# Two product groups at the start of a streaming-encoder step in full float32, their splits moved five groups later

## The chip, the core and the metric

The program runs on one core of a Trainium2 chip. The metric is device time in microseconds (us) from start to end of one execution; a smaller number is better. The engines named here are TensorE (PE in the profile; its weight loads stand apart as PEld), VectorE (DVE), ScalarE (ACT), GpSimd (POOL) and SyncE (SP, which issues most DMA transfers). Each engine works through its own instructions in the written order and waits where an instruction needs something that another engine or a transfer has not yet delivered.

## The reference

The reference is one inference step of a one-layer hybrid encoder on 1024 prompt tokens and 32 sample tokens (1056 in all), 1024 features wide, all in float32:

```python
h = rmsnorm(x, g_mix)
proj = h @ w_in
q, k, v, cb, cc, cx, ga, gc = jnp.split(proj, SPLITS, axis=-1)
y_attn = attend(q, k, v) @ w_attn_out          # stick-breaking attention, 8 heads of 64
conv_out, new_buf = causal_conv(cc * cx, conv_buf, conv_w)
y_conv = (cb * conv_out) @ w_conv_out
merged = jax.nn.sigmoid(ga) * y_attn + jax.nn.sigmoid(gc) * y_conv
x = x + merged @ w_o
f = jnp.square(jax.nn.relu(rmsnorm(x, g_ffn) @ w_up)) @ w_down
x = x + f
x = x + jax.nn.sigmoid(rmsnorm(x, g_ple) @ w_ple_gate) * (p @ w_ple)
```

The change lies in the first pieces of `h @ w_in`. The kernel multiplies `x * g_mix` with the weights and applies the row's norm to the result later, so the first products need only `x`, `g_mix` and `w_in`.

## The kernel before

**Split float32.** Nearly all large products are done in three fast products in place of a slow float32 one. An operand is split into a high part (written as `fp32r` by ScalarE) and a low part (the remainder, written as `fp32r` by VectorE). For each 128-feature piece TensorE then does high weight times high x (L371), high weight times low x (L372) and low weight times high x (L373), all added up in one PSUM tile. Those three lines are in `products`, and what it calls a group here is one call: 8 feature pieces, 24 matrix products of 128x128 weights with 264 tokens, one PSUM tile `ps_g`.

**The first stage.** `first_gates` (L1010 on) computes four output blocks of 128 columns for all 1056 tokens: `SETS[0]` (blocks 0 and 1, weights `i0`) and `SETS[1]` (weights `i1`). The tokens lie in four quarters of 264; quarters 0 and 1 are the first half (`near_` and `far_`), 2 and 3 the second half (`whole_`). That makes 16 groups, numbered 0 to 15 in this document as the loop's `n` has it: groups 0 and 1 are the two blocks of `i0` on quarter 0 (the near tokens), 2 and 3 on quarter 1 (the far tokens), 4 to 7 on quarters 2 and 3; groups 8 to 11 are `i1` on quarters 2 and 3, groups 12 to 15 `i1` on quarters 0 and 1.

**What feeds it.** SyncE loads, in this order: the first half of block 0's weights, the near tokens in four pieces of two features blocks each (the second half of block 0's weights after the second piece), the two halves of block 1's weights, the far tokens in four pieces, the second half of the tokens in four pieces, and whole weight blocks of the later sets (`fetch_in`, L115). The loop runs at record time, and the order in which it calls things is the order on each engine:

- `half_of(j, h)` splits one half of the weights of block `j`: a ScalarE cast (L1033) and a VectorE subtraction (L1034).
- `parts_x(h, c, fs)` splits token range `c` for the features blocks `fs`: per block one ScalarE scaling by `g_mix` that rounds (L693) and one VectorE remainder (L182, in the helper `mix`). On a quarter these are 128x264, on `whole_` 128x528.
- `out(s, i, t)` copies a finished PSUM tile to SBUF on ScalarE (L1017); it stands one group behind.
- From group 4 on the generator `sums_x` runs one step after each group; its first steps scale the second half of `x` in place (ScalarE, L701) and form differences (VectorE, also L182, named `x<-x` in the profile).
- At groups 6 and 7, `prepare_plain` splits the weights of `i1`: a ScalarE cast (L124) and a VectorE subtraction `wlo_i` (L125), each over a whole 128x1024 block. Group 8 is the first that uses them; its third product needs `wlo_i`.
- At group 8 `fetch_in(2)` and `prepare("i2")` come in: GpSimd forms four sums of weights (`steps` in `prepare`, all recorded under L252).

Ahead of group 0 TensorE does `IDLE` products of `ones` with `ones` (L1393, tile `ps_idle`) whose result nobody reads. Both weight and token tiles come from pools of fixed size; a load into a tile that was used before waits for its last reader.

## Time and profile before

| what | value |
|---|---|
| time, median of 3 runs | 1510.66 us (1510.4 to 1511.49) |
| the profiled execution's own time | 1511.53 us |
| its span, first to last instruction | 1509.8 us |
| TensorE busy in the span | 1494.7 us (99%) |
| VectorE, ScalarE, GpSimd busy | 1153.5, 791.5, 375.7 us |
| granted TensorE clock | 0.998 of full |

The prediction reads views of this one execution. The timeline gives, in order of time, rows of start, length, engine, source line, operation, `out<-in`, shape, how many equal ones were merged (x8), and in brackets how long the engine had been idle before and what ended that. A length is from the start of the first to the end of the last of a row; since an engine starts an instruction before the former one has fully ended, the distance from start to start is a little shorter than the length of one. The tile and line views give the smallest, median and largest duration of an instruction in nanoseconds and, for a DMA, the time from issue to landing. A row with `SPq` is the issue of a transfer, not the transfer.

### The profile page before, as it was taken

The page shows a single profiled execution, that of the slowest core. Times are in us where ns is not written, and L with a number is a line of the kernel's source. Part 1 is how long each engine was busy: PE and PEld are TensorE (multiplying, and loading weights), DVE is VectorE, ACT ScalarE, POOL GpSimd, SP SyncE. Part 2 cuts the span into 40 slices and gives each one's busy share as a digit, 9 for nine tenths or more (in the row PEclk, how much of TensorE's full clock was granted, in tenths as well). Part 3 has the DMA queues.
Part 4 walks back from the last instruction along what each step waited for, and adds up shares of the span by engine and source line. Part 5 has one row for each costly group of instructions (what it writes and reads, how often), then busy time and mean ns, then how long its engine had stood idle before and what let it go on. Part 6 is the DMA issues. An engine that isn't in the chain of part 4 may idle for free.

```text
span 1509.8 us, 29499 instructions
## 1 busy us (share of the span) xinstructions
PE 1494.7 (99%) x11580; PEld 1480.6 (98%) x11580; DVE 1153.5 (76%) x1624; ACT 791.5 (52%) x1567; POOL 375.7 (25%) x334
## 2 busy tenths in 40 slices
PE   9999999999999999999999999999999999999997
PEld 9999999999999999999999999999999999999997
DVE  7667689879578999876786676666689878879766
ACT  6654444445467767433475555555655433334655
POOL 1233335444121223003324433332000000000251
PEclk9999999999999999999999999999999999999999
DMA  6624425422678676654644334444879757855443
GB/s 245 211 73 170 163 64 198 154 84 96 220 247 276 182 170 143 220 196 162 234 163 149 136 137 150 157 150 157 312 281 289 244 187 239 295 186 166 141 129 123
DMA packets 116747, 275.52 MB, mean 182 GB/s; under 512 B 14048, under 2 KB 30048, under 8 KB 116608
## 3 DMA queue, kind: packets, MB, share of 16 engines
q1 hardware_dynamic: 112720, 260.44, 50.9%
q0 software_dynamic: 1728, 6.29, 2.5%
q10 hardware_dynamic: 2160, 6.91, 1.5%
q8 instruction: 91, 1.49, 0.4%
q14 instruction: 48, 0.39, 0.1%
HBM read 196.10 MB, written 85.88 MB: 187 GB/s over the span
## 4 chain that ended last, share of the span: by engine, by line
PE 92%; DVE 4%; DMA 1%; ACT 1%; issue 1%; SPq 0%; ACTq 0%; DVEq 0%
PE ps_dn L2000 6%; PE ps_dn L1999 6%; PE ps_dn L1998 6%; PE ps_A11i L371 4%; PE ps_A11i L372 4%; PE ps_A11i L373 4%; PE ps_A11u L372 4%; PE ps_A11u L371 4%; PE ps_A11u L373 4%; PE av L1278 2%; PE ps_S1i L373 2%; PE ps_S1i L372 2%; PE ps_S1i L371 2%; PE ps_wo L133 2%; PE ps_wo L135 2%; PE ps_wo L134 2%
## 5 line engine op out<-in xcount | busy, mean ns | idle before, releaser
L2000 PE MATMUL ps_dn<-fhP,wlo_dn 128*128 128x264 f32 x768 | 218.6, 285 | 0.0
L1999 PE MATMUL ps_dn<-flP,whi_dn 128*128 128x264 f32 x768 | 218.2, 284 | 0.2 <-DVE flP L1864 0.2
L1998 PE MATMUL ps_dn<-fhP,whi_dn 128*128 128x264 f32 x768 | 218.2, 284 | 0.0
L1999 PEld LDWEIGHTS ps_dn<-flP,whi_dn 128*128 128x128 f32 x768 | 144.4, 188 | 0.4 <-DVE flP L1864 0.4
L2000 PEld LDWEIGHTS ps_dn<-fhP,wlo_dn 128*128 128x128 f32 x768 | 144.5, 188 | 0.2 <-DVE wlo_dn L1848 0.2
L1998 PEld LDWEIGHTS ps_dn<-fhP,whi_dn 128*128 128x128 f32 x768 | 144.5, 188 | 0.0
L2213 POOL TENSOR_TENSOR xx<-xx,pgs 128x400 f32<-128x400 f32 (+1 forms) x17 | 20.0, 1183 | 281.4 <-DVE pgs L2212 281.4
L1223 DVE TENSOR_TENSOR_SCAN r<-r 128x128 f32<-128x128 f32 (+3 forms) x64 | 86.7, 1355 | 4.0 <-POOL r L1216 4.0
L371 PE MATMUL ps_A11i<-T,shS_i 128*128 128x264 f32 x288 | 82.5, 286 | 0.4 <-ACT u_i L515 0.4
L372 PE MATMUL ps_A11i<-T,shS_i 128*128 128x264 f32 x288 | 82.1, 285 | 0.0
L373 PE MATMUL ps_A11i<-T,slS_i 128*128 128x264 f32 x288 | 81.7, 284 | 0.0
L371 PE MATMUL ps_A11u<-T,shS_u 128*128 128x264 f32 x256 | 73.3, 286 | 0.0
L372 PE MATMUL ps_A11u<-T,shS_u 128*128 128x264 f32 x256 | 73.0, 285 | 0.0
L373 PE MATMUL ps_A11u<-T,slS_u 128*128 128x264 f32 x256 | 72.7, 284 | 0.0
L1216 POOL TENSOR_SCALAR_AFFINE_SELECT r<-r 128x128 f32<-128x128 f32 x64 | 35.8, 560 | 133.1 <-ACT r L1209 133.1
L1842 ACT CAST whi_dn<-raw_dn 128x1024 fp32r<-128x1024 f32 x31 | 32.6, 1052 | 66.2 <-PE ps_dn L1999 54.0
L135 PE MATMUL ps_wo<-mh,wlo_wo 128*128 128x352 f32 x192 | 62.0, 323 | 0.0
L1864 DVE TENSOR_TENSOR flP<-mrP,fhP 128x1056 fp32r<-128x1056 f32 x48 | 59.9, 1251 | 2.8 <-ACT fhP L1859 2.8
L134 PE MATMUL ps_wo<-ml,whi_wo 128*128 128x352 f32 x192 | 62.0, 323 | 0.0
L133 PE MATMUL ps_wo<-mh,whi_wo 128*128 128x352 f32 x192 | 61.7, 324 | 0.0
L250 DVE TENSOR_TENSOR slS_i<-s_i,shS_i 128x512 fp32r<-128x512 f32 x54 | 49.5, 917 | 13.1 <-ACT shS_i L191 12.8
L1263 DVE TENSOR_TENSOR at<-pa,at 128x512 fp32r<-128x512 f32 (+2 forms) x96 | 50.6, 548 | 11.4 <-ACT at L1262 10.6
(1704 smaller groups left out, 5794.8 us busy)
## 6 DMA issues: line engine op xcount, KB each, us to landing
raw_dn<-in_w_down_dram SPq DMA_DIRECT2D x59, 512.0 KB, 5.1
mrP<-mdT SPq DMA_DIRECT2D x32, 528.0 KB, 6.1
mdB<-m SPq DMA_DIRECT2D x48, 264.0 KB, 2.1
mrP<-mdB SPq DMA_DIRECT2D x24, 528.0 KB, 6.8
s<-gd SPq DMA_DIRECT2D x16, 528.0 KB, 5.3
mdT<-ta SPq DMA_DIRECT2D x32, 264.0 KB, 3.2
raw_pg<-in_w_ple_gate_dram SPq DMA_DIRECT2D x15, 512.0 KB, 3.5
gd<-m_i SPq DMA_DIRECT2D x12, 528.0 KB, 3.0
```

The lines of the kernel that those rows point to most:

```text
L133: nc.tensor.matmul(ps, wh, xh[k][:, cols], start=(k == order[0]), stop=False)
L134: nc.tensor.matmul(ps, wh, xl[k][:, cols], start=False, stop=False)
L135: nc.tensor.matmul(ps, wl, xh[k][:, cols], start=False, stop=(k == order[-1]))
L371: nc.tensor.matmul(p_, wh[:, k, :], h, start=new and n == 0, stop=False, **on)
L372: nc.tensor.matmul(p_, wh[:, k, :], l, start=False, stop=False, **on)
L373: nc.tensor.matmul(p_, wl[:, k, :], h, start=False, stop=z, **on)
L1223: nc.vector.tensor_tensor_scan(rev, rev, rev, 1.0, ALU.mult, ALU.bypass)
L1263: nc.vector.tensor_tensor(al, pt[:, :nb, :], ah.bitcast(F32), op=ALU.subtract)
L1864: dve(l, mraw.pop(v), opd[v].bitcast(F32), op=sub)
L1998: nc.tensor.matmul(ps, hi[:, j, :], oh, start=j == 0, stop=False)
L1999: nc.tensor.matmul(ps, hi[:, j, :], ol, start=False, stop=False)
L2000: nc.tensor.matmul(ps, lo[:, j, :], oh, start=False, stop=j == NP_ - 1)
```

## The change

Groups 0 and 1 no longer use split operands. A new function scales the near tokens on ScalarE into plain float32 tiles `xs`, and a second one multiplies these with the raw, unsplit weights in float32 products, 8 of them to a group. The splits of block 0's and 1's weights, and of the far tokens, are recorded at group 1, the far tokens now with the even feature blocks ahead of the odd ones. The near tokens are still split, since groups 12 to 15 use them, but at group 5. The idle products are 8, not 14.

```diff
-IDLE = 14
+IDLE = 8
...
+        xs = [blk(f"xs{h}", F32, [P, 4, TQ]) for h in range(2)]
+
+        def whole_x():
+            for f in range(8):
+                src = xw[0][f // 2][:, f % 2, near_]
+                nc.scalar.activation(xs[f // 4][:, f % 4, :], src, AF.Copy, scale=gmix[:, f : f + 1])
+
+        def whole_product(i):
+            p_ = group(f"ps_f{i}", TQ)
+            fs = (0, 2, 1, 3, 4, 5, 6, 7)
+            for f in fs:
+                w = raws["i0"][i][:, 4 * (f % 2) + f // 2, :]
+                nc.tensor.matmul(p_, w, xs[f // 4][:, f % 4, :], start=f == fs[0], stop=f == fs[-1])
+            return p_
...
+                whole_x()
+            elif n == 1:
                 half_of(0, 0)
-                parts_x(0, near_, (0, 1, 2, 3))
+                parts_x(0, far_, (0, 2, 4, 6))
                 half_of(0, 1)
-                parts_x(0, near_, (4, 5, 6, 7))
+                parts_x(0, far_, (1, 3, 5, 7))
                 half_of(1, 0)
                 half_of(1, 1)
-            elif n in (1, 3):
-                parts_x(n // 2, far_ if n == 1 else whole_)
+            elif n == 3:
+                parts_x(1, whole_)
+            elif n == 5:
+                parts_x(0, near_)
...
-            late.append(products(f"g{s_}{i}{t}", ((w[a], f"B1{c}"), (w[b], f"B2{c}")), quarters[t % 2]))
+            if n < 2:
+                late.append(whole_product(i))
+            else:
+                late.append(products(f"g{s_}{i}{t}", ((w[a], f"B1{c}"), (w[b], f"B2{c}")), quarters[t % 2]))
```

**ScalarE at the start of the program.** In the rows, `x00` to `x03` are the four pieces of the first half of the tokens (near and far columns of a piece have the same name), `x10` to `x13` those of the second half, `B11`, `B21` their split parts for even and odd feature blocks, `raw_i0_0` and `raw_i0_1` the weights of blocks 0 and 1. Before:

```order
L1033 CAST whi_i0_0_193<-raw_i0_0_88 128x512
L693 ACTIVATE B11_0_199<-x00_80,vecT_78 128x264
L693 ACTIVATE B21_00_202<-x00_80,vecT_78 128x264
...
L1033 CAST whi_i0_1_195<-raw_i0_1_89 128x512 x2
L693 ACTIVATE B11_0_199<-x00_80,vecT_78 128x264
L693 ACTIVATE B21_01_254<-x00_80,vecT_78 128x264
L693 ACTIVATE B11_1_205<-x01_81,vecT_78 128x264
...
L1017 COPY sg0_191<-ps_g000_227 128x264
L1017 COPY sg1_192<-ps_g010_270 128x264
L693 ACTIVATE B12_0_322<-x10_84,vecT_78 128x528
```

And now:

```order
L1026 ACTIVATE xs0_187<-x00_80,vecT_78 128x264 x2
...
L1026 ACTIVATE xs1_188<-x03_83,vecT_78 128x264 x2
L1048 CAST whi_i0_0_189<-raw_i0_0_88 128x512
L693 ACTIVATE B11_0_212<-x00_80,vecT_78 128x264
L693 ACTIVATE B11_1_215<-x01_81,vecT_78 128x264
L693 ACTIVATE B11_2_218<-x02_82,vecT_78 128x264
L693 ACTIVATE B11_3_221<-x03_83,vecT_78 128x264
L1048 CAST whi_i0_0_189<-raw_i0_0_88 128x512
L693 ACTIVATE B21_01_226<-x00_80,vecT_78 128x264
...
L1048 CAST whi_i0_1_191<-raw_i0_1_89 128x512 x2
L1017 COPY sg0_185<-ps_f0_201 128x264
```

The number of ScalarE instructions ahead of the splits of the second half (`B12_0`) is the same, 22 in all; the eight scalings into `xs` take the place of the eight near splits, and and the four even splits of the far tokens, one from each far piece, now stand ahead of the four odd ones and of three of the weight casts.

**VectorE between the second half's splits and the low part of the weights of `i1`.** Before:

```order
L182 SCALAR_TENSOR_TENSOR B22_3_343<-x13_87,vecT_78,B22_3_343 128x528
L182 SCALAR_TENSOR_TENSOR x10_84<-x10_84,vecT_78 128x528
L182 SCALAR_TENSOR_TENSOR x11_85<-x11_85,vecT_78 128x528
L182 SCALAR_TENSOR_TENSOR x12_86<-x12_86,vecT_78 128x528
L182 SCALAR_TENSOR_TENSOR x13_87<-x13_87,vecT_78 128x528
L182 SCALAR_TENSOR_TENSOR x10_84<-x00_80,vecT_78,x10_84 128x528
L182 SCALAR_TENSOR_TENSOR x11_85<-x01_81,vecT_78,x11_85 128x528
L125 TENSOR_TENSOR wlo_i1_0_461<-raw_i1_0_106,whi_i1_0_460 128x1024
```

And now:

```order
L182 SCALAR_TENSOR_TENSOR x11_85<-x11_85,vecT_78 128x528
L182 SCALAR_TENSOR_TENSOR B11_0_212<-x00_80,vecT_78,B11_0_212 128x264
...
L182 SCALAR_TENSOR_TENSOR B21_10_367<-x03_83,vecT_78,B21_10_367 128x264
L182 SCALAR_TENSOR_TENSOR x12_86<-x12_86,vecT_78 128x528
L182 SCALAR_TENSOR_TENSOR x13_87<-x13_87,vecT_78 128x528
L182 SCALAR_TENSOR_TENSOR x10_84<-x00_80,vecT_78,x10_84 128x528
L182 SCALAR_TENSOR_TENSOR x11_85<-x01_81,vecT_78,x11_85 128x528
L125 TENSOR_TENSOR wlo_i1_0_433<-raw_i1_0_106,whi_i1_0_432 128x1024
```

All eight low parts of the near tokens now stand between the second and the third difference of `sums_x`, ahead of `wlo_i` of group 8. From `wlo_i` on, the instructions of every engine stand in the order they had.

More of the change, by code (lines that the diff above doesn't have):

```diff
@@ L1035, in half_of @@
                     ws["i0"][f"A{j + 1}{h + 1}"] = hi, lo
+                whole_x()
+            elif n == 1:
                 half_of(0, 0)
-                parts_x(0, near_, (0, 1, 2, 3))
+                parts_x(0, far_, (0, 2, 4, 6))
                 half_of(0, 1)
-                parts_x(0, near_, (4, 5, 6, 7))
+                parts_x(0, far_, (1, 3, 5, 7))
                 half_of(1, 0)
                 half_of(1, 1)
-            elif n in (1, 3):
-                parts_x(n // 2, far_ if n == 1 else whole_)
+            elif n == 3:
+                parts_x(1, whole_)
+            elif n == 5:
+                parts_x(0, near_)
             elif n == 8:
                 m.extend(blk(f"sg{n}") for n in (2, 3))
-            w, c = ws[f"i{s_}"], t // 2 + 1
+            w, c = ws.get(f"i{s_}"), t // 2 + 1
             a, b = (("A11", "A12"), ("A21", "A22"))[i]
-            late.append(products(f"g{s_}{i}{t}", ((w[a], f"B1{c}"), (w[b], f"B2{c}")), quarters[t % 2]))
+            if n < 2:
+                late.append(whole_product(i))
+            else:
+                late.append(products(f"g{s_}{i}{t}", ((w[a], f"B1{c}"), (w[b], f"B2{c}")), quarters[t % 2]))
             if n:
```

## The prediction

> **What bounds the kernel now.** I read the page first, then the timeline of the first 60 us, engine by engine.
>
> ```profile
> PE 1494.7 (99%) x11580; PEld 1480.6 (98%) x11580; DVE 1153.5 (76%) x1624; ACT 791.5 (52%) x1567; POOL 375.7 (25%) x334
> PE 92%; DVE 4%; DMA 1%; ACT 1%; issue 1%; SPq 0%; ACTq 0%; DVEq 0%
> ```
>
> TensorE is busy for 99% of the span and has 92% of the chain that ended last. So a microsecond by which TensorE is late after the edited stage is a microsecond of the result, unless a later idle stretch takes it up; there is next to none. I therefore need one number: how much later or earlier TensorE is where the order of instructions becomes the old one again, at group 8.
>
> ```profile
> 6.11 0.36 PE L371 MATMUL ps_g<-B,whi_i 128*128 128x264 f32 x1
> ...
> 14.02 0.29 PE L371 MATMUL ps_g<-B,whi_i 128*128 128x264 f32 x1
> ...
> 22.79 0.28 PE L371 MATMUL ps_g<-B,whi_i 128*128 128x264 f32 x1
> ...
> 31.58 0.29 PE L371 MATMUL ps_g<-B,whi_i 128*128 128x264 f32 x1
> ...
> 32.24 0.39 PE L373 MATMUL ps_g<-B,wlo_i 128*128 128x264 f32 x1 [0.25 <-DVE wlo_i L125]
> ...
> 35.02 0.28 PE L371 MATMUL ps_g<-B,whi_i 128*128 128x264 f32 x1
> ```
>
> Counted by 24 products, these are the first products of groups 0, 2, 5, 8, then the third of group 8, and the first of group 9. From group 5 to 8 it is 8.79 us for 72 products, 0.122 each, 2.93 a group. Groups 0 and 1 took 7.91, so they lost some 2.05 to waits. Group 8 took 3.44: its third product waited for the low weights `wlo_i`. VectorE is thus already the last to arrive at group 8, before any change.
>
> **ScalarE.**
>
> ```profile
> 4.42 0.92 ACT L693 ACTIVATE B<-x,vecT 128x264 fp32r<-128x264 f32 x2 [0.20 <-DMA x<-in_xf_dram]
> 5.87 0.92 ACT L693 ACTIVATE B<-x,vecT 128x264 fp32r<-128x264 f32 x2 [0.53 <-DMA x<-in_xf_dram]
> ...
> 7.23 1.74 ACT L693 ACTIVATE B<-x,vecT 128x264 fp32r<-128x264 f32 x4
> 8.87 1.15 ACT L1033 CAST whi_i<-raw_i 128x512 fp32r<-128x512 f32 x2
> ...
> 14.22 0.38 ACT L1017 COPY sg<-ps_g 128x264 f32<-128x264 f32 x1 [0.45 <-PE ps_g L373]
> 14.49 5.12 ACT L693 ACTIVATE B<-x,vecT 128x528 fp32r<-128x528 f32 x8
> ...
> 20.34 1.37 ACT L701 ACTIVATE x<-x,vecT 128x528 f32<-128x528 f32 x2
> ```
>
> From start to start a 264-column scaling takes 0.41 (1.74 = 3 x 0.41 + 0.50), a cast 0.52 to 0.55, a copy 0.27, a 528-column scaling 0.63, the last of them 0.73. When the token pieces land:
>
> ```profile
> L635 SPq DMA_DIRECT2D x<-in_xf_dram x4: 418/448/469, 1.3 to 3.2; - x4
> ...
> DMA to landing us min/median/max: 3.1/4.3/4.7
> ```
>
> ```profile
> L635 SPq DMA_DIRECT2D x<-in_xf_dram x4: 435/516/678, 5.0 to 6.6; - x4
> ...
> DMA to landing us min/median/max: 5.1/5.5/5.8
> ```
>
> The first fence is the near pieces: the last lands at 3.2 + 4.7 = 7.9. The second is the far ones: the first lands at 5.0 + 5.1 = 10.1, the last at 6.6 + 5.8 = 12.4.
>
> **The change, part by part.** *Groups 0 and 1.* What a float32 product costs is shown once at full clock, for 352 columns:
>
> ```profile
> 879.26 0.76 PE L1692 MATMUL ps_ms<-ssq,ones 128*128 128x352 f32 x2
> ...
> L1692 PE MATMUL ps_ms<-ssq,ones x6: 457/458/460, 879.3 to 887.3; 128*128 128x352 f32 x6
> ```
>
> One product is two instructions, 0.76 - 0.46 = 0.30 apart; by columns 0.30 x 264/352 = 0.223, so 0.445 a product and 3.56 a group against 2.93: the two groups cost 1.3 us more TensorE work. In return only one thing has to precede a product, one scaling. The scalings keep the starts of the quoted rows (4.42, 5.87, 7.23 and on, each 0.41 apart, no cast between them), so they end in 8.87 + 0.1. The first product starts at 4.95, the second needs piece two and starts at 5.87 + 0.50 = 6.4, and with it seven products run on without a wait worth a tenth: group 0 ends at 6.4 + 7 x 0.445 = 9.5, group 1 at 13.1 (its weights had landed by 9.4, when their second cast ran before). Group 2 started at 14.02. **Gain here: 0.9.**
>
> *Idle products.* Eight in place of fourteen:
>
> ```profile
> 1.13 5.22 PE L1393 MATMUL ps_idle<-ones 128*128 128x128 f32 x28 [1.13 <-DVE eps_t L104]
> ...
> L1393 PE MATMUL ps_idle<-ones x15: 421/421/421, 1.7 to 4.7; 128*128 128x128 f32 x15
> ...
> L1393 PE MATMUL ps_idle<-ones x12: 275/275/421, 4.7 to 6.1; 128*128 128x128 f32 x12
> ```
>
> The first 15 stand 3.0/14 = 0.214 apart, the later ones 0.11: TensorE reaches full pace at about 4.9. Sixteen instructions end at 1.13 + 16 x 0.214 = 4.6, before anything can be multiplied, so the idle ones are in nobody's way and the six left out save nothing by themselves; fourteen would hold the first product until 6.1. Should full pace come later for it, groups 0 and 1 get slower, with a cover of 1.9 us that the next paragraphs give.
>
> *ScalarE's new order.* After the scalings: a cast, 8.97 to 9.5; then the even far splits, each of which needs another far piece, so the fourth starts no sooner than 12.4. Before, the eight far splits started at 10.14 in order of arrival and that wait was hidden. Behind the fourth: 0.41, the second cast 0.52, four odd splits 1.64, two casts 1.05, two copies 0.55. The splits of the second half begin at 12.4 + 4.17 = 16.6 in place of 14.49: **2.1 later.**
>
> ```profile
> 9.56 1.29 DVE L1034 TENSOR_TENSOR wlo_i<-raw_i,whi_i 128x512 fp32r<-128x512 f32 x2
> ...
> 12.79 1.29 DVE L182 SCALAR_TENSOR_TENSOR B<-x,vecT,B 128x264 fp32r<-128x264 f32 x3
> 15.27 5.53 DVE L182 SCALAR_TENSOR_TENSOR B<-x,vecT,B 128x528 fp32r<-128x528 f32 x8 [1.19 <-ACT B L693]
> 21.11 1.45 DVE L182 SCALAR_TENSOR_TENSOR x<-x,vecT 128x528 f32<-128x528 f32 x2 [0.32 <-ACT x L701]
> 24.03 3.57 DVE L182 SCALAR_TENSOR_TENSOR x<-x,vecT 128x528 f32<-128x528 f32 x2 [1.48 <-ACT x L701]
> 27.53 3.52 DVE L182 SCALAR_TENSOR_TENSOR x<-x,vecT,x 128x528 f32<-128x528 f32 x2
> 30.97 1.21 DVE L125 TENSOR_TENSOR wlo_i<-raw_i,whi_i 128x1024 fp32r<-128x1024 f32 x1
> ```
>
> Remainders take 0.40 at 264 columns and 0.68 at 528, start to start (0.76 + 7 x 0.68 = 5.53), low parts of half a weight block 0.6. The last odd far remainder ends near 15.8 and block 1's low parts near 17.0, each two casts or scalings behind ScalarE; groups 2 and 3, at 13.1 to 16.05 and on to 19.0, meet them with waits below 0.1. The remainders of the second half followed ScalarE by 0.78 (14.49, 15.27), so now they begin at 17.4, and the seventh (the last even one) ends at 17.4 + 6 x 0.68 + 0.76 = 22.2. In group 4 its product is the 11th; 14 are left: 22.2 + 14 x 0.122 = 23.9. Group 5 started at 22.79: **TensorE is now 1.1 late.** (Group 3 ends at 19.0 and group 4's ten products before it take 1.2: this is the cover of 22.2 - 20.3 = 1.9.) Groups 5, 6, 7 follow; group 8 starts at 23.9 + 8.8 = 32.7.
>
> *The eight near splits.* VectorE is free at 17.4 + 8 x 0.68 = 22.8. ScalarE: splits until 16.6 + 8 x 0.63 = 21.6, two copies, first scaling of `x` ends at 22.9. So the first two differences run 22.9 to 24.3 (before 21.11 to 22.5). Then it idled 1.48 until 24.03; now the eight remainders come, 3.2 us, then the four 528-column operations, 2.7. But GpSimd is at work:
>
> ```profile
> 24.03 1.29 POOL L252 TENSOR_TENSOR s_i<-raw_i,raw_i 128x512 f32<-128x512 f32 x1 [22.65 <-DMA raw_i<-in_w_in_dram]
> ...
> 28.83 1.65 POOL L252 TENSOR_TENSOR s_i<-s_i,raw_i 128x512 f32<-128x512 f32 x1
> ```
>
> Four such operations run in turns with VectorE's four from 24.03 to 30.97: 6.94 in place of 2.72, a toll of 4.2, about 1.05 for each of GpSimd's. Does a 264-column remainder pay it too? This kernel shows one of the same form, VectorE's row and GpSimd's beside it:
>
> ```profile
> 701.49 1.55 DVE L182 SCALAR_TENSOR_TENSOR B<-xr,vecT,B 128x264 fp32r<-128x264 f32 x1 [0.58 <-ACT B L1599]
> ```
>
> ```profile
> 701.47 1.29 POOL L252 TENSOR_TENSOR raw_u<-raw_u 128x512 f32<-128x512 f32 x1
> ```
>
> 1.55 in place of 0.49: yes, 1.07. So the toll is per GpSimd operation and stays 4.2 (bounds 0 and 8 x 1.07 = 8.6, which would need eight; there are four). `wlo_i` starts at 24.3 + 3.2 + 2.7 + 4.2 = 34.4 and ends at 35.6, in place of 32.18. Group 8's third product, ready at 32.9, goes 0.06 behind that as before, at 35.7 and not at 32.24: **3.4 late**, and with it, in order behind it, all of TensorE's work. The 1.1 of group 4 is contained in this, not added.
>
> *The clock in that wait.* TensorE stands for 2.8 us, longer than anywhere in this trace. The rows of the idle products show what a slow clock costs: half of the 3.8 us until full pace, 1.9. The stops inside group 0, 2.05 in pieces, left the products behind them 0.122 apart, so by the rows of this trace the sum stays 3.4. The Trainium skill (TensorE: Matmul & The Clock Gate, "Why this matters for your kernels") asks for no idle gap above about 3 us, since a window of idleness brings back half rate; 2.8 is just inside, and with a slightly longer stop the sum by that page would be 5.3.
>
> *Later.* The second `wlo_i` comes 2.5 us behind the first (as before, two differences and itself) and is needed by group 10, 5.9 after group 8's start: no wait. The near parts, ready at about 32, are first used by group 12. The two loads of set 2's weights go into the tiles of `raw_i0` and now wait on SyncE for their last low parts, until about 14 and 17 us. Behind them in SyncE's queue stands the store of block 0, not complete before group 6. They landed at 24.0 by GpSimd's row, in a queue of earlier loads, and I leave them there.
>
> **The sum**: 35.7 - 32.24 = 3.4 with the unrounded terms, against the profiled execution 1511.53 + 3.4 = 1514.9 (its span 1509.8 + 3.4 = 1513.2, with 1.7 around it). That execution is 0.9 above the median, so the forecast for a median is 1510.66 + 3.4 = **1514.1**.
>
> **The rivals.** *The toll is not paid.* If the short remainders slip between GpSimd's operations, `wlo_i` ends at 35.7 - 4.2 = 31.5, before group 8 starts. The point from which this decides is a toll below 1.2 in all. What is left is group 4's 1.1: 1511.8, not slower as far as this can be measured. For it: the operations are half as long. Against it: the row at 701.49.
>
> *GpSimd moves away.* The second load of set 2 took this long from issue to landing:
>
> ```profile
> raw_i<-in_w_in_dram SPq DMA_DIRECT2D x1, 512.0 KB, 11.5
> ```
>
> It now goes out at 17. If it needed 11.5 again, it would land at 28.6, not 24.0, and two of the four tolls would fall behind `wlo_i`: 35.7 - 2.1 + 1.0 (a turn of its own with GpSimd) = 34.6, so +2.3, 1513.0. Against it: it waited behind loads that were still arriving, and its place among them stays.
>
> *The clock falls.* If the stop in group 8 brings back the slow pace of the idle rows, 1.9 more is lost: 1516.0. The length of the stop decides. Against it: with 0.998 granted over the span, no stretch of this trace shows such a fall. (That about 3 us is the limit stands in the Trainium skill, TensorE: Matmul & The Clock Gate, "Why this matters for your kernels".)
>
> *The gain stays.* 0.9 of groups 0 and 1 arrives at the end, 1509.8. It would need `wlo_i` to end by 31.3 with eight more operations ahead of it on an engine that was last already. I see nothing that would do it.
>
> **How the numbers follow.** My forecast 0.71 (its own range 1513.3 to 1514.9, from 0.8 less to 0.8 more for the bounds on landings and toll), the toll 0.10, GpSimd 0.08, the clock 0.08, the gain 0.03. The range from 1511.7 to 1515.8 leaves out the last two, about one in ten. A measurement of this kernel tells about 0.2% from no change, 3.0 us. Four fifths of my forecast lie beyond that, 0.58, and the clock's 0.08: slower 0.66. The rest of the forecast with the toll, GpSimd and the gain make 0.32 for no change; 0.02 is left for faster.
>
> **What would show it.** In the changed profile: group 2 starting near 13.1; ScalarE idle for pieces of x between 9.5 and 12.4 and the 528-column splits starting near 16.6; group 5 near 23.9; eight 264-column remainders near 24 to 32 on VectorE, four of them about 1.45 apart; `wlo_i` starting near 34.4; one TensorE wait of 2.5 us or more at L373; group 9 near 38.5 in place of 35.02. I am wrong if `wlo_i` ends before 33, or if group 9 is late and the end is not.

## The result, and the profile after

The changed kernel takes 1517.76 us, median of 6 runs (1516.25 to 1519.12), against 1511.03 us for 6 runs of the kernel before beside them: ratio 1.0041, 95% interval 1.0031 to 1.0052. In a later measurement, unedited, it took 1516.97 us against 1511.87: 1.0039, 1.0026 to 1.0051. So the change makes the kernel 5 to 7 us slower. The forecast was 3.4 us, to 1514.1, with a range to 1515.8: the direction was right, the size was not.

The page of the changed kernel (profiled execution 1519.01 us, span 1517.3 us, granted clock 0.997) still shows a TensorE that is busy 99% of the span, in a longer span; more of the chain that ended last lies on VectorE and on transfers than before (4% and 1%).

```profile
PE 1498.5 (99%) x11552; PEld 1482.2 (98%) x11552; DVE 1153.7 (76%) x1624; ACT 794.5 (52%) x1575; POOL 376.7 (25%) x334
PE 88%; DVE 5%; DMA 3%; ACT 2%; issue 1%; SPq 0%; ACTq 0%; DVEq 0%
```

TensorE's timeline of the changed kernel. L1033 is the new float32 product. The rows from 13.51 on are the first products of groups 2, 5 and 8, the third of group 8, two behind it, and the first of group 9.

```profile
5.11 1.08 PE L1033 MATMUL ps_f<-xs,raw_i 128*128 128x264 f32 x2 [0.20 <-ACT xs L1026]
6.74 7.12 PE L1033 MATMUL ps_f<-xs,raw_i 128*128 128x264 f32 x30 [0.56 <-ACT xs L1026]
13.51 0.48 PE L371 MATMUL ps_g<-B,whi_i 128*128 128x264 f32 x1
...
24.42 0.28 PE L371 MATMUL ps_g<-B,whi_i 128*128 128x264 f32 x1
...
33.23 0.28 PE L371 MATMUL ps_g<-B,whi_i 128*128 128x264 f32 x1
...
36.01 0.39 PE L373 MATMUL ps_g<-B,wlo_i 128*128 128x264 f32 x1 [2.37 <-DVE wlo_i L125]
...
37.01 0.42 PE L373 MATMUL ps_g<-B,wlo_i 128*128 128x264 f32 x1
37.23 0.42 PE L371 MATMUL ps_g<-B,whi_i 128*128 128x264 f32 x1
...
40.32 0.29 PE L371 MATMUL ps_g<-B,whi_i 128*128 128x264 f32 x1
```

The reader is to see two things. The one long stop is where the forecast put it, at L373 of group 8, released by `wlo_i`. And behind it the products stand 0.22 apart in place of 0.12, so that group 9 starts 5.3 us after its old 35.02 though the third product of group 8 is only 3.8 after its old 32.24.

ScalarE of the changed kernel waits for far pieces, as worked out, and starts the 528-column splits at 16.94 (before 14.49):

```profile
9.33 0.60 ACT L1048 CAST whi_i<-raw_i 128x512 fp32r<-128x512 f32 x1
10.55 0.51 ACT L693 ACTIVATE B<-x,vecT 128x264 fp32r<-128x264 f32 x1 [0.62 <-DMA x<-in_xf_dram]
...
12.80 0.52 ACT L693 ACTIVATE B<-x,vecT 128x264 fp32r<-128x264 f32 x1 [0.22 <-DMA x<-in_xf_dram]
...
16.94 5.13 ACT L693 ACTIVATE B<-x,vecT 128x528 fp32r<-128x528 f32 x8
```

VectorE's queue ahead of `wlo_i` in the changed kernel, and GpSimd's four operations beside it:

```profile
23.27 1.45 DVE L182 SCALAR_TENSOR_TENSOR x<-x,vecT 128x528 f32<-128x528 f32 x2
24.64 7.46 DVE L182 SCALAR_TENSOR_TENSOR B<-x,vecT,B 128x264 fp32r<-128x264 f32 x8
32.02 1.43 DVE L182 SCALAR_TENSOR_TENSOR x<-x,vecT 128x528 f32<-128x528 f32 x2
33.38 1.44 DVE L182 SCALAR_TENSOR_TENSOR x<-x,vecT,x 128x528 f32<-128x528 f32 x2
34.74 1.21 DVE L125 TENSOR_TENSOR wlo_i<-raw_i,whi_i 128x1024 fp32r<-128x1024 f32 x1
```

```profile
24.35 1.52 POOL L252 TENSOR_TENSOR s_i<-raw_i,raw_i 128x512 f32<-128x512 f32 x1 [22.96 <-DMA raw_i<-in_w_in_dram]
...
28.83 1.36 POOL L252 TENSOR_TENSOR s_i<-s_i,raw_i 128x512 f32<-128x512 f32 x1
```

One line of the tile view has the smallest, median and largest duration of a remainder in ns:

```profile
L182 DVE SCALAR_TENSOR_TENSOR B<-x,vecT,B x24: 478/627/1519, 11.1 to 31.6; 128x264 fp32r<-128x264 f32 x16, 128x528 fp32r<-128x528 f32 x8
```

The eight near remainders take 7.46 where eight alone take 3.3 (the run with the sums on VectorE, below); the four 528-column operations behind them, which before ran in turns with GpSimd, now run at their own pace. From 23.27 to 34.74 are 11.5 us, the operations alone are 2 x 0.68 + 8 x 0.40 + 4 x 0.68 = 7.3: a toll of 4.2, the same as before the change, paid by other instructions.

| step | forecast | first profile | second profile (the unedited repeat) |
|---|---|---|---|
| group 2 starts | 13.1 | 13.51 | 13.05 |
| 528-column splits start | 16.6 | 16.94 | 16.64 |
| group 5 starts | 23.9 | 24.42 | 24.13 |
| `wlo_i` starts | 34.4 | 34.74 | 34.47 |
| third product of group 8 | 35.7 | 36.01 | 35.74 |
| group 9 starts | 38.5 | 40.32 | 39.87 |
| later at the last products, against the first profile of before | 3.4 | 7.45 | 5.43 |

Up to the third product of group 8 the second profile follows the forecast within 0.3; the first is some 0.3 later, since its last far split starts 0.3 later too (12.80 against 12.50 in the second profile). The two rows below that are what the forecast lacks.

### The profile page after: what moved, and what is told of

The parts are those of the page before. It is cut to its first block, busy times and chain, and to the rows that moved or that the text cites. A ratio compares the mean times of both kernels' runs of the same rounds, so it can differ in the third digit from the quotient of the medians.

```text
span 1517.3 us, 29447 instructions
## 1 busy us (share of the span) xinstructions
PE 1498.5 (99%) x11552; PEld 1482.2 (98%) x11552; DVE 1153.7 (76%) x1624; ACT 794.5 (52%) x1575; POOL 376.7 (25%) x334
## 4 chain that ended last, share of the span: by engine, by line
PE 88%; DVE 5%; DMA 3%; ACT 2%; issue 1%; SPq 0%; ACTq 0%; DVEq 0%
PE ps_dn L2022 6%; PE ps_dn L2021 6%; PE ps_dn L2020 6%; PE ps_A11u L372 4%; PE ps_A11u L371 4%; PE ps_A11u L373 4%; PE ps_A11i L371 4%; PE ps_A11i L372 4%; PE ps_A11i L373 4%; PE av L1300 2%; PE ps_wo L135 2%; PE ps_wo L133 2%; PE ps_wo L134 2%; PE ps_S1i L373 2%; PE ps_S1i L372 2%; PE ps_S1i L371 2%
## 5 line engine op out<-in xcount | busy, mean ns | idle before, releaser
L2235 POOL TENSOR_TENSOR xx<-xx,pgs 128x400 f32<-128x400 f32 (+1 forms) x17 | 20.0, 1184 | 281.4 <-DVE pgs L2234 281.4
L373 PE MATMUL ps_A11i<-T,slS_i 128*128 128x264 f32 x288 | 81.9, 284 | 0.0
L373 PE MATMUL ps_A11u<-T,slS_u 128*128 128x264 f32 x256 | 72.7, 284 | 0.0
```

The source lines that it names most:

```text
L373: nc.tensor.matmul(p_, wl[:, k, :], h, start=False, stop=z, **on)
```

## Experiments on VectorE's queue

Each edit is made to the changed kernel unless another is named, and no kernel here leaves out a part of the computation.

**Near splits behind `wlo_i`.**

```diff
-            elif n == 5:
-                parts_x(0, near_)
             elif n == 8:
+                parts_x(0, near_)
```

> The changed kernel, with the eight near splits (ScalarE scalings and VectorE remainders) recorded at group 8 in place of group 5, behind both wlo_i. Same work in all. Theory (the loss is VectorE's queue ahead of wlo_i, and the slow clock that the stop there brings): without the eight remainders the four 528-column differences start at 24.6 us, end with GpSimd's toll near 31.6, wlo_i ends near 32.9, before the third product of group 8 could go at 33.5; the stop of 2.4 us and the half-clock stretch behind it are gone, group 9 starts near 36.7 (before 35.02, after 40.32), and the kernel takes about 1511.0 + 1.7 = 1512.7; up to 1514.5 if the smaller losses after 80 us come with any lateness of TensorE. Rival 1 (the loss comes from the float32 groups and the shorter idle run themselves): it stays at 1517.8. Rival 2 (the near splits cost the same wherever they stand, since later steps then wait for VectorE): wlo_i in time, but a new wait of 2 to 4 us at group 10, at group 12 or at the next set of weights, and 1515 or more.

Measured: 1513.89 us, ratio to before 1.0020 (1.0011 to 1.0029). `wlo_i` ends at 32.29, there is no stop in group 8 and no slow stretch, and group 9 starts at 35.72, 0.7 late. So the place of the eight remainders, not the float32 groups, makes the stop. The whole is 2.9 over before, 1.2 more than expected; the section on what lies behind group 9 comes back to that.

**GpSimd's sums on VectorE.** The order of the near splits stays. Only the four sums of set `i2` change engine, and stand on VectorE behind both `wlo_i`.

```diff
-        lows = []
+        lows, sums = [], dve if s_ == "i2" else pool
...
-            0: [partial(pool, s3, a11, a21, op=sub)],
+            0: [partial(sums, s3, a11, a21, op=sub)],
```

(and so for steps 1 to 3.)

> The changed kernel, near splits where the change put them, with one edit: the four sums of weights of set i2 are done by VectorE (recorded behind both wlo_i) and not by GpSimd, so that GpSimd stands still while VectorE works through the near remainders. Theory (the toll of 4.2 us, paid to four GpSimd operations, is what makes wlo_i late): eight remainders at 0.40 and four differences at 0.68 run from 24.3 to 30.3, wlo_i ends near 31.5 in place of 35.7 to 35.95, before group 8 starts at 32.9 to 33.2; no stop, no half clock; group 9 is late by the 1.3 to 1.6 of group 5 alone and the kernel is about 2.3 over before with the smaller waits behind it. Rival (VectorE's own rate sets it: remainders near 1.5 us each whatever GpSimd does): wlo_i stays near 35.9, 5 to 6 over before.

VectorE's timeline of this kernel:

```profile
22.88 1.46 DVE L182 SCALAR_TENSOR_TENSOR x<-x,vecT 128x528 f32<-128x528 f32 x2
24.24 3.32 DVE L182 SCALAR_TENSOR_TENSOR B<-x,vecT,B 128x264 fp32r<-128x264 f32 x8
...
31.07 1.23 DVE L125 TENSOR_TENSOR wlo_i<-raw_i,whi_i 128x1024 fp32r<-128x1024 f32 x1 [0.60 <-ACT whi_i L124]
```

The same eight instructions take 3.32 in place of 7.46. The toll was GpSimd's: shown, not argued. `wlo_i` ends at 32.3, not 31.5, since it now waits for ScalarE's cast. The stop and the slow stretch are gone, and group 9 starts at 35.74. Time 1515.30, ratio 1.0024 (1.0015 to 1.0033), 1.5 us over the forecast. The Trainium skill (SBUF — State Buffer, "Who interferes with whom") has VectorE and GpSimd share one pair of ports as an exclusive lock; the rows agree, each of the four remainders lasting 1.52 beside GpSimd's 1.36 to 1.52, and 0.48 without.

The control puts the same four sums on VectorE in the kernel before.

> The kernel before with the same four sums on VectorE, the control for the run with them in the changed kernel. Theory: the differences no longer run in turns with GpSimd, wlo_i ends some 4 us earlier than 32.18, the wait of 0.25 in group 8 goes, and nothing else changes: before less 0.2, not to be told from before. Rival (VectorE is short of time behind group 8 with 2.5 us more work): 1 or more over before.

1512.49 against 1511.51, ratio 1.0006 (0.9997 to 1.0015): no difference that can be told, rather above than below. Taking away the toll is worth nothing where nobody waits for `wlo_i`.

**Far splits in order of arrival.**

```diff
-                parts_x(0, far_, (0, 2, 4, 6))
+                parts_x(0, far_, (0, 1, 2, 3))
...
-                parts_x(0, far_, (1, 3, 5, 7))
+                parts_x(0, far_, (4, 5, 6, 7))
```

> The changed kernel, with the far splits in the order of arrival (features blocks 0 to 3, then 4 to 7) as before the change; the near splits stay at group 5. Theory: ScalarE waits less for pieces, the 528-column splits start near 15.9 in place of 16.94, group 5 near 23.4 in place of 24.42, and VectorE's whole queue moves up by the same 1.0: wlo_i ends near 34.9, the third product of group 8 goes at 35.0 in place of 36.0. The stop there stays near 2.4 us, so the half-clock stretch stays too: 1.0 less than the changed kernel, about 1516.8. Rival (GpSimd's four operations and not the splits set when VectorE is done): group 5 at 23.4 but wlo_i still near 36, a stop of 3.4 us, 1517.8.

The 528-column splits start at 15.49, group 5 at 22.98, and the third product of group 8 at 34.57, 1.2 to 1.4 earlier than in the two profiles of the changed kernel: the order costs that much, and it passes through VectorE's queue to `wlo_i`, as claimed. The stop is 2.38 again, and the slow stretch comes again. The time, 1514.60, ratio 1.0023 (1.0013 to 1.0032), is 2.2 below the 1516.8 expected, a miss: group 9 starts at 38.59, 3.6 late, and this profile loses nothing more behind it, where the changed kernel's two lose 0.6 and 2.1.

**Both edits.**

> Both edits: near splits at group 8 and far splits in order of arrival. Theory: the lateness at group 5 is 0.6 (23.4 against 22.79) and nothing is added at group 8, so group 9 starts near 35.7 and the kernel takes 1511.0 + 0.7 = 1511.7, not to be told from before. If the float32 groups have a cost of their own: 1513 or more.

Group 9 starts at 35.27, 0.25 behind before and 0.4 earlier than expected; but the time is 1513.27, ratio 1.0013 (1.0004 to 1.0022), about 2 us over before and not 0.7. Again the loss at group 9 is explained and something behind it is not.

## Experiments on the clock

The windows view of the changed kernel, by periods of 3.41 us. The first number behind the stretch is its length, the next is TensorE's busy time with its count, the one that follows the five engines is the granted clock.

```profile
33.18:36.60 3.42, 1.05 (x9) 0.84 (x8) 3.42 (x6) 2.45 (x4) 0.00 (x0) 1.00 0.21 83
36.60:40.01 3.41, 3.41 (x18) 3.41 (x17) 3.41 (x6) 1.27 (x2) 0.00 (x0) 0.50 0.70 184
40.01:43.40 3.39, 3.39 (x30) 3.39 (x29) 2.85 (x4) 1.44 (x3) 1.65 (x2) 1.00 0.82 289
```

The clock is half for exactly the 3.41 us behind the stretch that holds the stop, and TensorE gets through 18 products there in place of 30. The first experiment fills the stop with work that nobody reads, ahead of group 8:

```diff
+                spare = tps.tile([P, 512], F32, tag="tp", name="ps_spare")
+                for _ in range(10):
+                    nc.tensor.matmul(spare[:, :P], ones, ones, start=True, stop=True)
```

> The changed kernel, with ten idle products of ones with ones (128 columns, about 0.22 us each at full clock, result not read) on TensorE just ahead of group 8, so that TensorE works through most of its wait for wlo_i. Nothing on VectorE moves: wlo_i ends near 35.95 and the third product of group 8 goes near 36.0 as in the changed kernel. Theory (the stop of 2.4 us brought half the clock for 3.4 us, which cost 1.6): the products behind it stand 0.122 apart, group 9 starts near 38.7 in place of 40.3, and the kernel is 1.6 faster with more work, about 1516.2. Rival (the slow stretch has another cause, or did not happen in the timed runs): no change, 1517.8, or 0.1 to 0.3 more.

In its profile no half clock follows, and group 9 starts at 38.42, although `wlo_i` ends within 0.4 of where it ended. But the time was 1517.10, ratio 1.0042 (1.0029 to 1.0054): no gain. A repeat, and the changed kernel twice more, once with 14 idle products at the start:

> The changed kernel with ten idle products ahead of group 8 once more, for a second profile and five more times. Theory: no half clock behind group 8 in this profile either, group 9 near 38.4 to 38.8 in place of 40.3 and 39.8 (the two profiles of the changed kernel), and with the earlier times pooled about 1 us under the changed kernel. Rival: no difference in time, as the first five times had it; then what the half clock costs at group 9 must be given back or lost elsewhere.

> The changed kernel once more, unedited, for a second profile and the timed runs beside the others. Theory: wlo_i again ends near 35.9 and TensorE stops for 2.4 us ahead of it; the half clock behind it comes again if it hangs on the length of the stop (group 9 at 40.3), and is absent in some executions if it hangs on where the stop falls in the clock's own period of 3.41 us (group 9 at 38.7). The later waits: 0.6 to 0.9 near 82 to 85 us again; the 0.9 near 236 us not always, since it needs one GpSimd operation to fall beside one VectorE operation.

> The changed kernel with 14 idle products in place of 8. Theory (whatever happens to groups 0 and 1 is hidden by the wait for wlo_i in group 8): the float32 products start at 6.1 instead of 5.1, group 2 starts up to 0.8 later, and group 9 stands where it stood: 1517.8 within 0.7. Rival (the shorter idle run is what costs, by a late full pace): 1515 or less.

| kernel | stop | half clock behind it | third product of group 8 | group 9 | ratio (95%) |
|---|---|---|---|---|---|
| changed, first | 2.37 | yes | 36.01 | 40.32 | 1.0041 (1.0031 to 1.0052) |
| changed, again | 2.40 | yes | 35.74 | 39.87 | 1.0039 (1.0026 to 1.0051) |
| changed, 14 idle | 2.38 | no | 35.72 | 38.51 | 1.0032 (1.0020 to 1.0045) |
| ten spare, first | 0.16 | no | 35.64 | 38.42 | 1.0042 (1.0029 to 1.0054) |
| ten spare, again | 0.16 | no | 35.63 | 38.42 | 1.0032 (1.0019 to 1.0044) |

From the third product to group 9 it is 2.8 us without the half clock, as before the change (35.02 - 32.24), and 4.1 to 4.3 with it: 1.4 (1.2 in the run with the far splits in order, 34.57 to 38.59). With 14 idle products the third product comes at the same time as with 8, so the shorter idle run costs the changed kernel nothing at group 8, as expected. The same stop of 2.4 us brought the half clock twice and once not. The windows say why. Of the repeat, and of the kernel with 14 idle products:

```profile
31.93:35.34 3.41, 1.41 (x12) 1.20 (x10) 3.41 (x5) 2.33 (x4) 0.00 (x0) 1.00 0.40 161
35.34:38.76 3.42, 3.02 (x13) 3.02 (x14) 3.42 (x6) 1.42 (x3) 0.00 (x0) 0.50 0.50 153
```

```profile
31.20:34.61 3.41, 2.14 (x18) 1.93 (x16) 3.41 (x7) 1.81 (x4) 0.00 (x0) 1.00 0.41 163
34.61:38.02 3.41, 2.31 (x19) 2.31 (x19) 3.41 (x4) 2.13 (x4) 0.00 (x0) 1.00 0.34 112
```

In the first a single period holds 2.0 us of the stop, TensorE was busy for 1.41 of 3.41, and the next period runs at half clock. In the second the border of the periods (7.31, where full pace came, plus eight times 3.41) cuts the stop in two, TensorE was busy for 2.14 and 2.31, and nothing happens. So the length of the stop alone does not decide; where it lies against the periods does.

The times of these five do not separate the half clock's 1.4 from nothing. So the stop was made too long to miss a period, by 16 small additions on VectorE ahead of the first `wlo_i`, and filled in a second kernel.

```diff
+                if n == 6:
+                    scratch = cpool.tile([P, P], F32, name="scratch")
+                    for _ in range(16):
+                        dve(scratch, ones, ident, op=add)
                 prepare_plain("i1", n - 6)
```

> The changed kernel with 16 additions of 128x128 on VectorE (into a tile that nobody reads) right ahead of the first wlo_i, about 3 us: TensorE's stop in group 8 grows from 2.4 to some 5.5 us. Theory (a period of 3.41 us of which TensorE stands still for more than about half brings half the clock in the next one; with 2.0 us of 3.41 it came, with 1.27 it did not): wherever the periods fall, one of them is idle for at least 2.8 us, so half the clock comes in every execution and costs about 1.5: group 9 near 38.5 + 3.1 + 1.5 = 43.1. Rival (the half clock costs nothing in the end): see the next run.

> The same, with 25 idle products of ones with ones ahead of group 8, some 5.4 us at full clock, in the stop. VectorE's work is the same. Theory: no half clock, group 9 near 41.6, and the time 1.5 less than that of the run with the empty stop. Rival: group 9 earlier but the same time within 0.5, because later waits take back what TensorE gains.

This pair failed as a test: 1522.70 and 1523.39, ratios 1.0073 (1.0059 to 1.0087) and 1.0077 (1.0063 to 1.0091). The additions took 5 us, not 3, so that 25 products left 1.9 us of the stop empty, and the half clock came in both. The second kernel's windows are of use all the same:

```profile
38.50:41.91 3.41, 1.52 (x13) 1.30 (x12) 3.31 (x7) 0.35 (x1) 0.00 (x0) 1.00 0.05 8
41.91:45.32 3.41, 3.41 (x17) 3.41 (x17) 3.41 (x6) 0.92 (x2) 0.00 (x0) 0.50 0.66 214
```

A stop of 1.89 us is enough if it lies within one period. The pair again, with 34 products, and 14 idle ones at the start of both:

> The changed kernel with the 16 additions ahead of the first wlo_i, a stop of 6 to 7 us in group 8, and 14 idle products at the start. Theory: half the clock in every execution, and all of group 8 behind the stop at half pace, 1.5 to 2.4 us lost against the run with the filled stop.

> The same with 34 idle products ahead of group 8 (about 7.3 us at full clock), result not read, so that TensorE stops for less than 1 us there. VectorE's work is the same. Theory: no half clock; wlo_i at the same time within 0.5, the products behind it 0.12 apart, and the time 1.5 to 2.4 less than that of the run with the empty stop. Rival: the same time within 0.7.

TensorE's timeline with the empty stop, and with the filled one; the last row of each is group 9:

```profile
40.84 0.59 PE L373 MATMUL ps_g<-B,wlo_i 128*128 128x264 f32 x1 [7.49 <-DVE wlo_i L125]
41.22 0.42 PE L371 MATMUL ps_g<-B,whi_i 128*128 128x264 f32 x1
...
45.84 0.32 PE L371 MATMUL ps_g<-B,whi_i 128*128 128x264 f32 x1
```

```profile
41.20 0.39 PE L373 MATMUL ps_g<-B,wlo_i 128*128 128x264 f32 x1
41.42 0.28 PE L371 MATMUL ps_g<-B,whi_i 128*128 128x264 f32 x1
...
43.98 0.28 PE L371 MATMUL ps_g<-B,whi_i 128*128 128x264 f32 x1
```

5.0 against 2.8 us from the third product to group 9. The third product comes 0.4 later in the filled kernel, so group 9 gains 1.9. In the two profiles the last products start at 1513.45 and 1511.72, so that 1.7 of it arrives. In time: 1521.87 (1521.57 to 1523.76) against 1521.00 (1519.83 to 1521.33); each of the five filled runs lies below each of the six empty ones, by 0.9 in the medians and 1.5 in the means, where 1.5 to 2.4 was expected. The ratios, 1.0067 (1.0054 to 1.0079) and 1.0057 (1.0044 to 1.0070), overlap. So the half clock is paid for at the end too; how much of the 1.9 arrives there, the times tell only to about a microsecond.

## Experiments on what lies behind group 9

**TensorE late by itself.** The kernel before with 17 idle products ahead of group 8 (the edit of the spare products, in the other kernel).

> The kernel before with 17 idle products of ones with ones (about 3.7 us at full clock, result not read) on TensorE ahead of group 8. Nothing of VectorE's or ScalarE's own work changes, and TensorE never stops, so neither the queue ahead of wlo_i nor the clock plays a part. Theory (a microsecond by which TensorE is late at group 9 is a microsecond of the result): 3.5 late at group 9 (0.2 of it covered by the wait that was there) and about 1511.0 + 3.5 = 1514.5. Rival 1 (lateness by itself brings the further waits near 82 to 85 and 236 us that the changed kernel shows, 0.9 and 0.9): 1515.5 to 1516.5. Rival 2 (a wait for a transfer further back, 1.3 us near 445 us in the kernel before, takes up a part): 1513.3.

Group 9 starts at 38.19, 3.2 late. The time is 1515.22 against 1511.87, 3.4 over, ratio 1.0023 (1.0013 to 1.0032). A microsecond at group 9 is a microsecond at the end, within what this measurement tells; neither rival is needed.

**The kernel before, twice more.** The changed kernel's profile has two more stops that the first profile of before has not, or has shorter:

```profile
91.38 0.39 PE L371 MATMUL ps_A11i<-T,shS_i 128*128 128x264 f32 x1 [0.77 <-ACT u_i L515]
...
243.15 0.39 PE L373 MATMUL ps_S1i<-B,slS_i 128*128 128x264 f32 x1 [0.92 <-DVE slS_i L250]
```

> The kernel before, unedited, for a second profile. If the waits near 82 to 85 us hang on how fast single transfers of the norm's rows land (4.0 us for the sixth in the profile before and in the one with TensorE late, 4.5 to 5.8 in the others), a second profile of the same kernel can show them too, 0.4 or more over the first at 86 us. If they belong to the changes, this profile is level with the first there within 0.1.

> The kernel before, unedited, for a third profile: as for the second. Also the small increments: the same products, without any wait above 0.1, took 0.1 to 1.8 us more over the span in the other profiles than in the first; if that is of the execution and not of the edits, it is as large between profiles of the same kernel.

TensorE's row of the second profile of the kernel before, and ScalarE's 15 us ahead of it:

```profile
85.99 0.39 PE L371 MATMUL ps_A11i<-T,shS_i 128*128 128x264 f32 x1 [0.75 <-ACT u_i L515]
```

```profile
70.85 1.06 ACT L772 ACTIVATE xr<-xr 128x1024 f32<-128x1024 f32 x1 [0.76 <-DMA xr<-in_xr__dram]
```

The unedited kernel has the stop at L515 too, 0.75 and 0.77 in its further profiles and 0.39 in the first. It hangs on how fast the norm's rows land, not on the change. Both profiles gain as much back near 445 us, where the first waited 1.27 for a transfer, and end within 0.05 of the first. The single profile of before had a quiet stretch at 85 and a long wait at 445. The stop at 243 is of the execution as well: it is in the first profile of the changed kernel and not in the second, one reason why the two end 2 us apart.

**A part that does repeat.** Two products far apart, in the first profile of the kernel before and in that of the changed kernel:

```profile
461.00 0.34 PE L1207 MATMUL z<-ks,q 128*128 128x384 f32 x1
...
1501.95 0.25 PE L2248 MATMUL ps_rows<-ones,pq 128*128 128x1 f32 x1
```

```profile
467.56 0.34 PE L1229 MATMUL z<-ks,q 128*128 128x384 f32 x1
...
1509.40 0.25 PE L2270 MATMUL ps_rows<-ones,pq 128*128 128x1 f32 x1
```

1040.95 us before, 1041.84 after, with the same instructions in the same order. The same two products in the other profiles:

| kernel | first | second | between |
|---|---|---|---|
| before, second and third profile | 460.85, 460.88 | 1501.91, 1501.90 | 1041.06, 1041.02 |
| before, 8 idle | 463.20 | 1504.14 | 1040.94 |
| before, TensorE late | 463.94 | 1504.86 | 1040.92 |
| before, sums on VectorE | 461.48 | 1503.35 | 1041.87 |
| changed, again | 465.63 | 1507.38 | 1041.75 |
| changed, 14 idle | 464.57 | 1506.28 | 1041.71 |
| changed, ten spare, twice | 465.15, 464.67 | 1506.91, 1506.47 | 1041.76, 1041.80 |
| changed, far splits in order | 464.48 | 1505.58 | 1041.10 |
| changed, near splits at group 8 | 461.60 | 1503.90 | 1042.30 |
| changed, sums on VectorE | 461.99 | 1504.44 | 1042.45 |
| changed, both edits | 461.62 | 1504.42 | 1042.80 |
| candidate (last experiment below) | 460.77 | 1502.04 | 1041.27 |

One program repeats itself within about 0.1; between programs the stretch moves by up to 1.9. In the changed kernel the 0.8 come in steps below 0.1 us, far from the edit. They belong to that program and not to the float32 groups as such: with nothing but the far splits in another order 0.15 is left of them, and the sums on VectorE bring 0.9 without the change. (In the kernel with both edits 1.3 of its 1.85 lie at three products, near 1178, 1184 and 1190 us.) The cause stays open.

This is also the larger part of what the first section of experiments left unexplained. Their profiles lose 1.25 (near splits at group 8), 1.8 (sums on VectorE) and 2.2 (both edits) between group 9 and the last products, and 1.35, 1.5 and 1.85 of it in this stretch; the kernel with the far splits in order loses 0.15 here and 0.06 in all.

**The shorter idle run alone.** The kernel before with `IDLE = 8`.

> The kernel before with one edit, 8 idle products in place of 14; no float32 groups, no moved split. Theory (the six idle products less change nothing by themselves): group 0 starts about 1.0 earlier (5.1), waits longer for its pieces, and group 2 starts within 0.3 of 14.02: the time is that of before, 1511.0, within 0.6. Rival (TensorE reaches full pace only after a stretch of about 3.4 us without a stop; one profile of the changed kernel with spare products had it at 10.2 us): with waits inside groups 0 and 1 and no idle products under them, full pace can come as late as 8 to 10 us; the products until then take twice as long, group 2 starts 1 to 2 us late, nothing behind it takes that up, and the time is 1512 to 1513.

1512.78 against 1511.87, ratio 1.0008 (0.9999 to 1.0017): not told from no change. Its profile shows the rival's mechanism: products at half pace until 13.2.

```profile
12.55 0.42 PE L371 MATMUL ps_g<-B,whi_i 128*128 128x264 f32 x1
12.78 0.42 PE L372 MATMUL ps_g<-B,whi_i 128*128 128x264 f32 x1
...
13.32 0.28 PE L372 MATMUL ps_g<-B,whi_i 128*128 128x264 f32 x1
13.45 0.28 PE L373 MATMUL ps_g<-B,wlo_i 128*128 128x264 f32 x1
```

Group 2 starts at 15.74 there (before 14.02, 14.40 and 14.30 in three profiles), group 9 at 36.23, 1.2 late. In the profiles of the other kernels with 8 idle products full pace came anywhere from 4.4 to 13.3. In the changed kernel the stop at group 8 hides this; where the stop is gone (near splits at group 8, sums on VectorE) it is no longer hidden. That may be why their medians lie 0.4 and 1.3 above their own profiled executions, in both of which full pace came early (4.7 and 6.4). No run separates this.

**A candidate.** Near splits at group 8, the casts of three weight halves ahead of the far splits, these in order of arrival, the sums on VectorE, 11 idle products:

```diff
                 half_of(0, 0)
-                parts_x(0, far_, (0, 2, 4, 6))
                 half_of(0, 1)
-                parts_x(0, far_, (1, 3, 5, 7))
                 half_of(1, 0)
+                parts_x(0, far_)
                 half_of(1, 1)
```

> The float32 groups with everything else arranged around them: near splits at group 8, three weight casts ahead of the far splits (ScalarE has to wait for the far pieces there), the far splits in order of arrival, the sums of i2 on VectorE, 11 idle products. Theory (each loss that the runs showed has its cause in one of these places): the 528-column splits start near 14.7, no stop in group 4, wlo_i ends well before group 8, and the gain of groups 0 and 1 (0.5 to 0.9) is still there at group 9, which starts at 34.2 to 34.6 in place of 35.02; the time is that of before less 0.5, which cannot be told from before. Rival (the later near splits or a late transfer of the norm's rows cost the 0.8 to 1.4 between 82 and 85 us that four profiles show): 0.3 to 1 over before.

1511.76 against 1511.51, ratio 1.0000 (0.9991 to 1.0009). In its profile the 528-column splits start at 14.59, `wlo_i` ends at 30.73 and group 9 starts at 34.18, 0.8 ahead of before: the gain of the float32 groups does reach group 9 when nothing takes it away. It cannot be told at the end. This undoes the loss of the change, and it is no faster than the kernel before.

## Why the prediction was right and wrong

- **Groups 0 and 1, gain 0.9**: right. Group 2 at 13.05 and 13.51 against 13.1; the latter, of the first profile, by a later full pace (5.9 against 4.6) and later pieces. That full pace might come later was named; that it can come as late as 13 was not.
- **ScalarE's new order, 2.1 later, group 5 at 23.9**: right in kind and within 0.2 to 0.5. The run in order of arrival gives back the 1.2 to 1.4 that it costs at `wlo_i`.
- **The eight near splits, toll unchanged at 4.2, `wlo_i` at 34.4, third product at 35.7**: right within 0.3, and shown by taking away either side, the remainders or GpSimd. The rivals that the toll is not paid or that GpSimd moves away did not occur.
- **"Group 9 near 38.5", with the clock's fall as a rival at 0.08**: here the prediction failed. The step was "2.8 is just inside": I judged the stop by its length against a limit of about 3 us. The stops were 2.4, shorter than worked out, and the half clock came in both profiles of the changed kernel, since what counted was how much of one period of 3.41 us the stop filled. It cost 1.4 at group 9, not the 1.9 of the rival. "No stretch of this trace shows such a fall" was a wrong reading too. The granted clock of 0.998 in the profile of before does hold a fall, at the program's end, in windows laid on the periods:

```profile
1500.05:1503.46 3.41, 2.26 (x21) 2.18 (x19) 2.50 (x9) 2.70 (x5) 0.00 (x0) 1.00 0.00 0
1503.46:1506.87 3.41, 0.00 (x0) 0.00 (x0) 1.62 (x6) 1.74 (x3) 0.00 (x0) 0.50 0.35 139
```

TensorE has nothing left to do there, so this fall costs nothing. But it comes after only 1.15 us of idleness, and that spoke against a limit of 3 us. The cost of a stop was an unknown, and its upper end, 1.9 us, belonged inside the range.

- **"Later ... no wait", a microsecond late is a microsecond of the result**: right for the passing on (3.2 at group 9, 3.4 at the end), incomplete for the rest. The forecast put everything behind group 9 at nothing; the changed program loses 0.8 more in small steps between the two products at 461 and 1502 us, which no row of the profile of before could have shown, and the first profile held a stop of 0.9 near 243 us by chance.
- **The sum.** Third product of group 8 3.5 to 3.8 late, half clock 1.4 when it comes, the small steps 0.8: 5.7 to 6.0, against 5.1 and 6.7 in the medians and 5.4 at the last products of the second profile. The forecast held the first term alone (its 35.7 - 32.24 is 3.46, rounded down to 3.4). Neither missing term takes the forecast out of its range by itself: 1514.1 becomes 1515.5 with the half clock and 1514.9 with the small steps, and 1516.3 with both, where the range ended at 1515.8. The rest, up to the 6.7 of the first median, no run explains. The chance for slower, 0.66, was if anything too low.

## What to carry to other kernels

Work that is moved away from one wait lands ahead of another: before deferring it, look for the engine that was last already at the next stage, here VectorE with 0.25 us of wait at group 8, and put the deferred work behind what that stage waits for. Price a stop of TensorE by the share of a clock period that it may fill and not by its length alone, and give the slow period behind it a chance of its own whenever the stop is near half a period. Before reading a small stop in the changed profile as a consequence, take a second profile of the kernel before: here two of them showed the same stop.

## What the runs showed of the hardware

- The clock is granted by periods of 3.41 us. In each of the six profiles in which it fell at group 8, the fall came a whole number of periods (7, 9 or 11) after full pace, as at 36.60 after 5.88. Half clock followed where TensorE was busy for 1.05, 1.23, 1.41 and 1.52 us of one (31 to 45%, stops of 1.89 to 2.40 us), and not where it was busy for 2.14 or 2.31 (63 and 68%, a stop of 2.38 cut by the border) or for 2.07 (61%, the changed kernel from 19.53 on). No limit in per cent follows from this: at the program's end, where the last products are one column wide, the clock fell behind periods with 2.03 (changed) and 2.26 (before), so the busy time of the rows is not all that counts. The Trainium skill (TensorE: Matmul & The Clock Gate, "Why this matters for your kernels") allows gaps to about 3 us; these stops of 1.9 to 2.4 us differ from it, and the measurement decides.
- The start of the periods against the program's start varies between executions (full pace at 5.88 and at 4.62 in the two profiles of the changed kernel). So the same stop of 2.4 us was punished in three profiles (the changed kernel twice, far splits in order) and not in a fourth (14 idle products). Full pace came at 4.4 to 13.3 us in these profiles with 8 idle products, at 4.8 to 7.3 with 14.
- A VectorE operation that runs in turns with GpSimd pays for GpSimd's operation whatever its own length: the four 264-column remainders beside GpSimd's rows started 1.44 apart against 0.40, and halving the operations did not halve the toll.
